# Loads and multiply-adds of the modulation vectors, recorded one step per weight tile of an MLP, with a sixth of the accumulator at a time

## The chip, the cores and the metric

One Trainium2 chip, one of its cores. The time is that of the whole program on the device, in microseconds, the median of several runs.

## The reference

Two blocks of two layers each, in float32, for 512 tokens of width 1024. The first block has an attention with selected keys, a squared-ReLU MLP, an attention with decay, a second MLP. The second block has modulated layers, and its modulation vectors depend on the small input `c` alone, not on the tokens:

```python
cond = jax.nn.silu(c)                                  # [1, 1024]
for i in range(DEPTH):                                 # 2 layers
    mod = cond @ ada_w[i] + ada_b[i]                   # [1024] x [1024, 6144]
    sh1, sc1, g1, sh2, sc2, g2 = jnp.split(mod, N_MOD, axis=-1)
    h = modulate(rmsnorm(x, norm1_g[i]), sh1, sc1)
    ...                                                # attention or gated MLP, added with g1
    h = modulate(rmsnorm(x, norm2_g[i]), sh2, sc2)
    x = x + g2[:, None, :] * sq_relu_mlp_2(h, mlp_w_in[i], mlp_w_out[i])
def sq_relu_mlp(xn, w_up, w_down):
    return jnp.square(jax.nn.relu(xn @ w_up)) @ w_down
```

`ada_w[i]` is 1024 x 6144 float32, 24 MB for each layer: as much as 48 weight tiles of the products.

## The kernel before

**Layout.** The activations lie with the features on the 128 partitions and the 512 tokens along the row: `h` is eight tiles of 128 x 512. A product is computed by weight tiles of 128 output features (`fm`): one load `wr` of 512 KB on SP's queue, a split of it in a high part `wh` (ScalarE) and a low part `wl` (VectorE), then 24 matmuls (8 slices of the inputs, three products each) into one bank of PSUM. There are two buffers `wr` and three each of `wh` and `wl`.

**An MLP** (`mlp`) has 64 such tiles, in four chunks: eight up tiles, then eight down tiles that use them. Behind an up tile VectorE evacuates the bank (`t`: ReLU times 1/rms), ScalarE squares it (`a`) and takes its high part (`ah`), VectorE its low part (`al`). A down tile's 24 matmuls go through the eight `ah`, `al` of the chunk in order, so its last three need those of the chunk's last up tile. Behind a down tile VectorE adds the bank to `h`.

**The modulation vectors.** `ada(0)` is handed to the MLP of the first layer, `ada(1)` to that of the second, as `side`. For each sixth `q` of the 6144 columns and each of eight slices `k` of the 1024 rows, it loads 512 KB (`adaw`, two buffers) on SP's queue; VectorE multiplies its two halves of 512 columns by `silu(c)` (a factor of each partition) and adds them to the accumulator `ada`, 128 x 6144. When all is added up, TensorE transposes the accumulator in 48 pieces of 128 columns, four to a bank `po`, and VectorE sums each bank over the partitions into `mod` (12 sums of 128 x 4). The vectors are used in the second block only.

**What sets the order.** The program is first recorded (`Sched.record`), each instruction with a number, its place in the record plus a bias (`later(n)` adds n). `Sched.order` then plays a list schedule with fixed durations: each engine, whenever it is free in that play, starts the ready instruction of the lowest number; one that needs a tile waits until a buffer of it is free. The instructions are emitted in that order and each engine's queue runs strictly in it; SP's queue holds all loads. On the chip an engine waits at its next instruction until its inputs are there, even where a later one could go. The instructions of `side` are recorded ahead of the MLP's first tile, with a bias of 1600: they give way to some 51 weight tiles.

Of the kernel before, what the change touches and what calls it, by code (L numbers as in the profile page):

```python
# [14 lines left out]
ALU = mybir.AluOpType  # L15
AX = mybir.AxisListType
PSUM = bass.MemoryType.PSUM

P = 128          # partitions, tokens of a block, features of a tile
S = 512          # tokens  # L20
D = 1024
HALVES = slice(0, S // 2), slice(S // 2, S)
KD = D // P      # feature tiles of the model width
NB = S // P      # token blocks
# [7 lines left out]
# columns of the packed per-feature vectors  # L32
# [10 lines left out]
class View:  # L43
    """a part of a tile that is not placed yet; slices and reshapes are replayed on the real one"""
# [33 lines left out]
    def bitcast(self, *a):  # L78
        """to a type of the same size"""
        return View(self.tile, self.steps + (("bitcast", a, {}),), self.box, self.flat)  # L80
# [30 lines left out]
class VPool:  # L111
    def __init__(self, sched, name, bufs, space, before, below):
        self.sched, self.name, self.bufs, self.space = sched, name, bufs, space
        self.before = before      # pools whose room it takes over
        self.below = below
        self.left = 0             # operations not emitted yet
        self.shared = None
        self.open_ = None
        self.slots = {}
# [5 lines left out]
# ns from the end of an instruction to the start of one that needs it  # L125
# [28 lines left out]
class Sched:  # L154
    """Records the program, orders each engine's instructions by a list schedule
    (ready instruction of lowest number first), then emits them in that order."""
# [28 lines left out]
    @contextmanager  # L185
    def later(self, n):
        """instructions that give way to the next n of the program"""
        self.bias += n
        yield
        self.bias -= n  # L190

    @contextmanager
    def after(self):
        """instructions that wait for the one before them"""
        self.gate = len(self.ops) - 1
        yield
        self.gate = None

    def record(self, eng, name, args, kw):
# [17 lines left out]
        if name == "matmul":  # L217
            # the sums of a bank one after the other
            t = outs[0].tile
            if kw["start"]:  # L220
                preds.update(t.sums)
            t.sums = {o.i}
# [19 lines left out]
    def cost(o, outs, ins):  # L242
        """ns that the engine is held, and ns until the result is there"""
# [29 lines left out]
    def order(self):  # L273
# [7 lines left out]
        parked = []               # wait for pools to be shut  # L281
# [23 lines left out]
        def room(p, q):  # L305
            if not q["free"]:
                return False
            # the first slot of a tag is its own, the others are shared by all tags of the pool
            return p.shared is None or not q["used"] or p.shared > sum(max(0, x["used"] - 1) for x in p.slots.values())
# [11 lines left out]
        while ev:  # L321
# [11 lines left out]
            while again:  # L333
                again = False
                for e, heap in ready.items():
                    while heap and busy[e] <= now:
# [15 lines left out]
                        if e == "tensor":  # L352
                            # the array runs at half its clock for a while after a pause
                            if now - busy[e] > 2500:
                                cold = now + 4000
                            if now < cold:
                                dur *= 2
# [62 lines left out]
class Norm:  # L420
    """h / rms(h) * gs + sh in two parts, by halves of the tokens; twice: of h / rms(h) * g_final"""
# [8 lines left out]
    def add(self, k, c=slice(0, S)):  # L430
        """the squares of a tile of h (times the gain) to their sums"""
# [5 lines left out]
        if half and c != self.part:  # L437
            # the squares of a half take turns in the halves of a tile
            self.part, self.n, self.sq = c, 0, net.t(net.np_, "sq", [P, S], bufs=1)
# [13 lines left out]
    def split(self, c):  # L453
# [10 lines left out]
        if self.twice:  # L464
            # 1/rms(h) / rms(h / rms(h) * g) = (mean((h g)^2) + eps (mean(h^2) + eps))^-1/2
            m2 = net.t(net.np_, "m2", [P, 2])
            nc.vector.tensor_scalar(m2, ms, EPS, 1.0, ALU.mult, ALU.mult)
            nc.vector.scalar_tensor_tensor(m2, ps[:, n + 4 : n + 8 : 2], 1.0 / D, m2, ALU.mult, ALU.add)
            nc.gpsimd.tensor_tensor(r, m2, net.mhalf[:, :2], ALU.pow)
            with net.sched.later(1000):  # L470
                nc.gpsimd.tensor_tensor(self.r[:, b0 : b0 + 2], ms, net.mhalf[:, :2], ALU.pow)
        else:
            nc.gpsimd.tensor_tensor(r, ms, net.mhalf[:, :2], ALU.pow)
# [16 lines left out]
class Net:  # L490
    def __init__(self, ctx, tc, I, out, stop=None):
# [6 lines left out]
        self.pp.shared = 4        # and a bank for each of 4 tags  # L498
# [34 lines left out]
    def weight(self, src, n):  # L533
        """src: [128, n] in DRAM; returns its high and low part"""
# [18 lines left out]
    def fm(self, src, xh, xl, w=None):  # L553
        """one tile of 128 output features, all tokens"""
# [8 lines left out]
    def tm(self, src, xh, xl, evac, banks=("mm", "mm", "lg", "tp")):  # L563
        """a strip of output features with the tokens on partitions; src: [u, 128, kk, n]"""
# [17 lines left out]
    def squares(self, col=None):  # L582
        """sums of the squares of h (times a gain) over the features: [token, 2 * block]"""
# [16 lines left out]
    def rms(self):  # L600
        """1/rms of the columns of h: [token, block], and spread over all partitions"""
# [35 lines left out]
    def last(self, src, xh, xl, gate, norm):  # L637
        """the product that completes h, and the norm of h; the end of both goes by halves of the tokens"""
# [20 lines left out]
    def first(self, src, xh, xl):  # L659
        """the first three tiles of a product, by halves of the tokens"""  # L660
# [13 lines left out]
    def mlp(self, xh, xl, w_up, w_down, rb=None, gate=None, side=None, norm=None):  # L674
        nc = self.nc
        with self.tc.tile_pool(name=self.name("mlp"), bufs=2) as mp:
            if side is not None:
                with self.sched.later(1600):
                    side(mp)
            head = [] if rb is not None else self.first([w_up[j] for j in range(3)], xh, xl)  # L680
            for c in range(DFF // D):
                ah, al = [], []
                for j in range(KD):
# [12 lines left out]
                    al.append(l_)  # L696
                if c < DFF // D - 1:
                    for k in range(KD):
                        self.residual(k, self.fm(w_down[c, k], ah, al), gate)
                else:  # L700
                    self.last([w_down[c, k] for k in range(KD)], ah, al, gate, norm)

# [1 line left out]
    def rope(self, pool, ps, cos, sin, eng, n=P, q=None, ceng=None):  # L704
        """ps * cos + (its halves of each head exchanged) * sin, in SBUF; the first n rows, repeated"""
# [14 lines left out]
    def stacks(self, pool, tag, s, bufs=None):  # L720
        """for the two heads of s: [high; low] and [low; high] along the partitions"""
# [9 lines left out]
    def doubles(self, pool, tag, s, scale):  # L731
        """for the two heads of s, scaled: [high; high] and [low; low]"""
# [13 lines left out]
    def softmax(self, pool, npr, lhs, rhs, W, masks, extra, rows, on_act=False):  # L746
        """rows of probabilities of one head, block after block; W: block of queries to its number of keys;
        lhs, rhs: pairs of operands whose products add up to the logits; rows: a factor of each row of them;
        on_act: which engine divides by the sums"""
# [32 lines left out]
    def turned(self, pool, nth, pr, W, b):  # L782
        """the probabilities of the keys of block b with the keys on partitions, in two parts, and their columns"""
# [16 lines left out]
    def heads(self, pool, npr, nth, lhs, rhs, v, o, masks=None, extra=(None, None), causal=True, rows=(None, None), blocks=range(NB), narrow=False, on_act=False):  # L800
        """two heads: their softmax times v, one above the other, in two parts to o.
        narrow: the products of the parts of v one after the other, not in the two halves of the array's columns"""
# [32 lines left out]
    def half_out(self, w, o, c):  # L835
        """adds the product of o for half of the tokens to h"""
# [11 lines left out]
    def layer_a(self, first):  # L848
# [6 lines left out]
        with ExitStack() as c1:  # L855
# [7 lines left out]
            # scores of the keys, then what is added to the logits  # L863
# [7 lines left out]
            with tc.tile_pool(name="ai", bufs=2) as ip:  # L871
# [37 lines left out]
                def top(i):  # L909
                    """keeps the 128 largest scores of each row: the others get NEG"""  # L910
# [38 lines left out]
    def layer_b(self):  # L949
# [4 lines left out]
        with ExitStack() as c1:  # L954
# [30 lines left out]
            with tc.tile_pool(name="bc", bufs=1) as bp:  # L985
                # log(sigmoid(z)) = min(z, 0) - log(1 + exp(-|z|)), and its sums over the tokens so far
# [60 lines left out]
    def layer_c(self, x, gate, norm):  # L1047
# [8 lines left out]
        with ExitStack() as c1:  # L1056
# [14 lines left out]
            def inverse(ps, st):  # L1071
                """1/rms of each of the two heads of a tile: [token, 2 * block + head]; by way of the bank st"""
# [140 lines left out]
    def ada(self, i):  # L1213
        nc, I = self.nc, self.I

        def side(pool):
            acc = self.t(pool, "ada", [P, 6 * D], bufs=1)
            for q in range(6):
                for k in range(KD):
# [3 lines left out]
                    for s in (0, 512):  # L1223
                        a = acc[:, q * D + s : q * D + s + 512]
# [4 lines left out]
            m = self.mod[i]  # L1229
            for j in range(0, 48, NB):  # L1230
                ps = self.po()
                for b in range(NB):
                    nc.tensor.transpose(ps[:, b * P : (b + 1) * P], acc[:, (j + b) * P : (j + b + 1) * P], self.ident)
                nc.vector.tensor_reduce(m[:, j : j + NB], ps.rearrange("p (b k) -> p b k", b=NB), AX.X, ALU.add)
# [105 lines left out]
def _layout(a):  # L1340
    """the inputs as the program reads them: tiled, permuted, packed"""

    def fm(w, kk=8):
        """[K, N] to [K/(128 kk), N/128, 128, kk, 128]"""
        k, n = w.shape
        return w.reshape(k // (P * kk), kk, P, n // P, P).transpose(0, 3, 2, 1, 4)

    def tm(w, kk, n):
        """[1024, N] to [N/n, 8/kk, 128, kk, n]"""
# [69 lines left out]
```

## Time and profile before

| | |
|---|---|
| median of 3 runs | 2642.7 us (2639.9 to 2642.72) |
| profiled execution | its span is 2640.9 us, first to last instruction; no other time of it is given |
| busy, share of the span | VectorE 1577.0 us (60%), ScalarE 1159.9 us (44%), GpSimd 467.8 us (18%) |
| mean granted TensorE clock | 0.990 |
| hardware DMA queue | 290.18 MB |

The profile is of one execution; its start times are microseconds from the first instruction. A group of a view names output and inputs as `out<-in`; all instructions have line 413, that of the emitting loop, so they are told apart by their tiles. `PE` is TensorE's matmul, `DVE` VectorE, `ACT` ScalarE, `SPq` the queue of the loads. The MLP with `ada(0)` begins near 265 us, that with `ada(1)` near 890 us.

### The profile page before, as it was taken

To read this page: it belongs to the slowest core of one execution; us is meant where nothing else is said; L and a number is where in the kernel's file an instruction comes from. 1 tells how busy PE (TensorE), PEld (TensorE's weight loads), DVE (VectorE), ACT (ScalarE), POOL (GpSimd) and SP (SyncE) were. 2 spreads that over 40 slices of the span, in tenths; PEclk is the share of its full clock that TensorE was granted. 3 is DMA by queue.
4 is the path that set the end of the run, shared out by engine and by line. 5 is a ranking of instruction groups with operands and counts; after the bars stand their busy time and mean duration, and the time that the engine had idled before them with its cause. 6 is when DMAs were issued, how large, how long until landed. Compare 5 with 4: busy or idle time off the path is not lost.

```text
span 2640.9 us, 34588 instructions
## 1 busy us (share of the span) xinstructions
PE 2570.4 (97%) x12998; PEld 2173.2 (82%) x12998; DVE 1577.0 (60%) x2667; ACT 1159.9 (44%) x2096; POOL 467.8 (18%) x628
## 2 busy tenths in 40 slices
PE   8989998999999998999999999999999999999999
PEld 6769787888888886888876888888998888888887
DVE  7998875455468777435698544434546654644433
ACT  5678322334477423323687433323435443523322
POOL 3773000000075000000686200000202210200000
PEclk9999999999999999999999999999999999999999
DMA  4222784223231576222211132222333332222222
GB/s 148 87 69 84 253 263 142 96 88 108 88 89 57 190 253 210 98 99 84 96 47 35 65 110 98 96 96 88 99 108 120 103 100 90 87 103 96 96 97 95
DMA packets 92056, 292.39 MB, mean 111 GB/s; under 512 B 11760, under 2 KB 16112, under 8 KB 91888
## 3 DMA queue, kind: packets, MB, share of 16 engines
q1 hardware_dynamic: 91888, 290.18, 32.8%
q8 instruction: 102, 1.67, 0.2%
q14 instruction: 66, 0.54, 0.1%
HBM read 277.28 MB, written 2.10 MB: 106 GB/s over the span
## 4 chain that ended last, share of the span: by engine, by line
PE 75%; DVE 10%; DMA 8%; ACT 3%; issue 2%; POOL 2%; SPq 0%; DVEq 0%; ACTq 0%; POOLq 0%
PE mm L413 64%; DMA adaw<-in_ada_w 7%; PE lg L413 4%; PE tp L413 4%; PE po L413 3%; DVE ada L413 2%; DVE mask L413 1%; DVE st L413 1%; ACT pr L413 1%; DVE tl L413 1%; POOL pr L413 1%; DVE m L413 1%; DVE acc L413 1%; ACT st L413 1%; ACT th L413 1%
## 5 line engine op out<-in xcount | busy, mean ns | idle before, releaser
L413 ACT ACTIVATE wh<-wr 128x1024 fp32r<-128x1024 f32 (+2 forms) x480 | 449.0, 940 | 1047.1 <-PE mm L413 865.3
L413 PE MATMUL mm<-xh,wh 128*128 128x512 f32 (+1 forms) x1640 | 627.8, 384 | 7.4 <-ACT wh L413 7.2
L413 DVE TENSOR_TENSOR wl<-wr,wh 128x1024 fp32r<-128x1024 f32 (+1 forms) x382 | 452.4, 1185 | 303.2 <-ACT wh L413 297.1
L413 PE MATMUL mm<-xh,wl 128*128 128x512 f32 (+1 forms) x1640 | 627.2, 383 | 1.3 <-DVE wl L413 0.9
L413 PE MATMUL mm<-xl,wh 128*128 128x512 f32 (+1 forms) x1640 | 627.0, 383 | 0.6 <-POOL xl L413 0.4
L413 PE MATMUL mm<-ah,wh 128*128 128x512 f32 (+1 forms) x1072 | 409.4, 382 | 16.9 <-ACT ah L413 16.9
L413 PE MATMUL mm<-al,wh 128*128 128x512 f32 (+1 forms) x1072 | 409.9, 382 | 0.7 <-DVE al L413 0.7
L413 PE MATMUL mm<-ah,wl 128*128 128x512 f32 (+1 forms) x1072 | 408.8, 381 | 1.1 <-DVE wl L413 1.1
L413 PEld LDWEIGHTS mm<-xh,wh 128*128 128x128 f32 x1640 | 311.6, 190 | 61.5 <-ACT wh L413 7.2
L413 PEld LDWEIGHTS mm<-xh,wl 128*128 128x128 f32 x1640 | 312.0, 190 | 59.7 <-DVE wl L413 3.5
L413 PEld LDWEIGHTS mm<-xl,wh 128*128 128x128 f32 x1640 | 312.5, 191 | 55.7 <-POOL xl L413 1.2
L413 PEld LDWEIGHTS mm<-ah,wh 128*128 128x128 f32 x1072 | 202.6, 189 | 58.3 <-ACT ah L413 20.0
L413 PEld LDWEIGHTS mm<-al,wh 128*128 128x128 f32 x1072 | 202.6, 189 | 41.2 <-DVE al L413 3.0
L413 PEld LDWEIGHTS mm<-ah,wl 128*128 128x128 f32 x1072 | 202.8, 189 | 39.9 <-DVE wl L413 2.0
L413 DVE SCALAR_TENSOR_TENSOR h<-mm,mod,h 128x512 f32<-128x512 f32 (+1 forms) x113 | 79.7, 707 | 260.3 <-PE mm L413 260.2
L413 POOL TENSOR_TENSOR wl<-wr,wh 128x512 fp32r<-128x512 f32 x98 | 133.1, 1368 | 144.9 <-ACT wh L413 138.4
L413 DVE SCALAR_TENSOR_TENSOR ada<-adaw,cs,ada 128x512 f32<-128x512 f32 x168 | 119.0, 748 | 43.2 <-DMA adaw<-in_ada_w 42.4
L413 DVE TENSOR_TENSOR h<-mm,h 128x512 f32<-128x512 f32 (+1 forms) x91 | 56.5, 624 | 147.0 <-PE mm L413 147.0
L413 PE MATMUL tp<-ident,pr 128*128 128x128 f32 x576 | 115.0, 278 | 7.3 <-POOL pr L413 3.4
L413 POOL TENSOR_SCALAR pr<-pr,rs 128x512 f32<-128x512 f32 (+3 forms) x168 | 110.3, 667 | 48.4 <-DVE rs L413 34.5
L413 ACT ACTIVATE ah<-a 128x512 fp32r<-128x512 f32 x128 | 80.9, 632 | 83.7 <-DVE a L413 81.6
L413 POOL TENSOR_TENSOR r<-ms,mhalf 128x2 f32<-128x2 f32 (+1 forms) x10 | 9.3, 934 | 606.9 <-DVE ms L413 545.7
(259 smaller groups left out, 4087.6 us busy)
## 6 DMA issues: line engine op xcount, KB each, us to landing
adaw<-in_ada_w SPq DMA_DIRECT2D x96, 512.0 KB, 4.5
wr<-in_w_up SPq DMA_DIRECT2D x64, 512.0 KB, 3.5
wr<-in_w_down SPq DMA_DIRECT2D x64, 512.0 KB, 3.5
wr<-in_w_in SPq DMA_DIRECT2D x64, 512.0 KB, 3.4
wr<-in_w_out SPq DMA_DIRECT2D x64, 512.0 KB, 3.5
wr<-in_w_gu SPq DMA_DIRECT2D x24, 512.0 KB, 3.5
wr<-in_w_gv SPq DMA_DIRECT2D x32, 384.0 KB, 3.0
wr<-in_w_go SPq DMA_DIRECT2D x32, 384.0 KB, 2.9
```

Of the source, the lines that this page charges most:

```text
L413: getattr(getattr(self.nc, o.eng), o.name)(*args, **kw)
```

## The change

`side` becomes a generator. Each step of it is one load `adaw` with its two multiply-adds; the last step of a sixth also has the transposes and sums of that sixth. `mlp` runs one step behind each of its tiles 1 to 55 (counted from 1), but not behind each eighth, so the steps are recorded between the tiles and get their numbers, with no bias. That makes 49 calls, for 48 steps and the short end (bias and gains). The accumulator `ada` is 128 x 1024, for one sixth, and there are two of them (the pool's `bufs=2`), where there was one of 128 x 6144. Comments are removed elsewhere.

```diff
     def mlp(self, xh, xl, w_up, w_down, rb=None, gate=None, side=None, norm=None):
         nc = self.nc
         with self.tc.tile_pool(name=self.name("mlp"), bufs=2) as mp:
-            if side is not None:
-                with self.sched.later(1600):
-                    side(mp)
+            side = None if side is None else side(mp)
+            tiles = 0
+
+            def step():
+
+                nonlocal tiles
+                tiles += 1
+                if side is not None and tiles % 8:
+                    next(side, None)
+
             head = [] if rb is not None else self.first([w_up[j] for j in range(3)], xh, xl)
...
                     ah.append(h_)
                     al.append(l_)
+                    step()
                 if c < DFF // D - 1:
                     for k in range(KD):
                         self.residual(k, self.fm(w_down[c, k], ah, al), gate)
+                        step()
                 else:
+                    for _ in side or ():
+                        pass
                     self.last([w_down[c, k] for k in range(KD)], ah, al, gate, norm)
...
         def side(pool):
-            acc = self.t(pool, "ada", [P, 6 * D], bufs=1)
+            m = self.mod[i]
             for q in range(6):
+                acc = self.t(pool, "ada", [P, D])
                 for k in range(KD):
...
-                        a = acc[:, q * D + s : q * D + s + 512]
+                        a = acc[:, s : s + 512]
...
-            m = self.mod[i]
-            for j in range(0, 48, NB):
-                ps = self.po()
-                for b in range(NB):
-                    nc.tensor.transpose(ps[:, b * P : (b + 1) * P], acc[:, (j + b) * P : (j + b + 1) * P], self.ident)
-                nc.vector.tensor_reduce(m[:, j : j + NB], ps.rearrange("p (b k) -> p b k", b=NB), AX.X, ALU.add)
+                    if k < KD - 1:
+                        yield
+                for j in range(0, KD, NB):
+                    ps = self.po()
+                    for b in range(NB):
+                        nc.tensor.transpose(ps[:, b * P : (b + 1) * P], acc[:, (j + b) * P : (j + b + 1) * P], self.ident)
+                    o = q * KD + j
+                    nc.vector.tensor_reduce(m[:, o : o + NB], ps.rearrange("p (b k) -> p b k", b=NB), AX.X, ALU.add)
+                yield
```

## Rows read from the trace of the kernel before

**Rows 1.** The page: TensorE's busy time; the chain of waits by line; the loads.
```profile
PE 2570.4 (97%) x12998; PEld 2173.2 (82%) x12998; DVE 1577.0 (60%) x2667; ACT 1159.9 (44%) x2096; POOL 467.8 (18%) x628
...
PE mm L413 64%; DMA adaw<-in_ada_w 7%; PE lg L413 4%; PE tp L413 4%; PE po L413 3%; DVE ada L413 2%; DVE mask L413 1%; DVE st L413 1%; ACT pr L413 1%; DVE tl L413 1%; POOL pr L413 1%; DVE m L413 1%; DVE acc L413 1%; ACT st L413 1%; ACT th L413 1%
...
adaw<-in_ada_w SPq DMA_DIRECT2D x96, 512.0 KB, 4.5
```

**Rows 2.** Windows of 20 us: length, busy us (instructions) by engine, clock, DMA.
```profile
300.00:320.00 20.00, 17.46 (x76) 13.92 (x75) 15.86 (x22) 7.26 (x10) 0.00 (x0) 1.00 0.78 248
400.00:420.00 20.00, 12.74 (x41) 8.56 (x40) 16.89 (x23) 6.74 (x9) 0.00 (x0) 0.74 0.66 210
420.00:440.00 20.00, 20.00 (x90) 16.56 (x89) 5.85 (x7) 3.52 (x4) 0.00 (x0) 1.00 0.28 104
...
1020.00:1040.00 20.00, 12.41 (x47) 8.47 (x45) 16.85 (x23) 7.51 (x11) 0.00 (x0) 0.84 0.66 214
```

**Rows 3.** VectorE's timeline, quiet part: start us, length us, instruction [idle before].
```profile
461.66 0.69 DVE L413 SCALAR_TENSOR_TENSOR t<-mm,y 128x512 f32<-128x512 f32 x1 [3.34 <-PE mm L413]
...
548.70 0.69 DVE L413 SCALAR_TENSOR_TENSOR t<-mm,y 128x512 f32<-128x512 f32 x1 [3.34 <-PE mm L413]
```

**Rows 4.** VectorE's timeline: `t` of tiles 1, 7, 23; then 1, 7, 32.
```profile
277.90 0.69 DVE L413 SCALAR_TENSOR_TENSOR t<-mm,y 128x512 f32<-128x512 f32 x1 [0.36 <-PE mm L413]
...
315.52 0.68 DVE L413 SCALAR_TENSOR_TENSOR t<-mm,y 128x512 f32<-128x512 f32 x1
...
412.98 0.68 DVE L413 SCALAR_TENSOR_TENSOR t<-mm,y 128x512 f32<-128x512 f32 x1
...
903.05 0.68 DVE L413 SCALAR_TENSOR_TENSOR t<-mm,y 128x512 f32<-128x512 f32 x1
...
939.50 0.68 DVE L413 SCALAR_TENSOR_TENSOR t<-mm,y 128x512 f32<-128x512 f32 x1
...
1086.25 0.69 DVE L413 SCALAR_TENSOR_TENSOR t<-mm,y 128x512 f32<-128x512 f32 x1 [3.35 <-PE mm L413]
```

**Rows 5.** TensorE's timeline at the end of tile 8, in both MLPs.
```profile
314.87 0.39 PE L413 MATMUL mm<-ah,wl 128*128 128x512 f32 x1
...
318.64 0.39 PE L413 MATMUL mm<-ah,wl 128*128 128x512 f32 x1
...
939.87 0.39 PE L413 MATMUL mm<-ah,wl 128*128 128x512 f32 x1
...
942.62 0.39 PE L413 MATMUL mm<-ah,wl 128*128 128x512 f32 x1
```

**Rows 6.** Instructions on the tile `ada`: one group; windows (PE, PEld, DVE).
```profile
L413 DVE SCALAR_TENSOR_TENSOR ada<-adaw,cs,ada x168: 736/747/754, 271.2 to 1036.8; 128x512 f32<-128x512 f32 x168
...
260.00:315.50 55.50, 0.00 (x0) 0.00 (x0) 20.07 (x30) 1.00 0.76 254
315.50:363.50 48.00, 0.00 (x0) 0.00 (x0) 21.50 (x33) 1.00 0.81 263
```

**Rows 7.** Longer windows of the first MLP; last columns clock, DMA share, GB/s.
```profile
265.00:317.00 52.00, 50.26 (x230) 41.36 (x228) 43.38 (x62) 21.52 (x29) 1.48 (x1) 1.00 0.77 253
317.00:396.00 79.00, 77.84 (x341) 63.92 (x341) 60.48 (x84) 19.89 (x24) 0.00 (x0) 1.00 0.80 260
...
417.00:563.00 146.00, 146.00 (x640) 120.79 (x640) 58.98 (x66) 41.04 (x49) 0.53 (x1) 0.99 0.27 96
```

**Rows 8.** Waits, 255 to 430 us: us in total, times, longest; then SP's queue.
```profile
DVE ada L413 <- DMA adaw<-in_ada_w: 25.7, 29, 1.8
...
SPq L413 <- DVE ada L413: 64.0, 46, 2.1
```

**Rows 9.** TensorE's transposes of `ada`: the group; two of its timeline.
```profile
L413 PE MATMUL po<-ident,ada x96: 270/272/275, 564.8 to 1205.1; 128*128 128x128 f32 x96
...
573.07 0.60 PE L413 MATMUL po<-ident,ada 128*128 128x128 f32 x4
...
573.74 0.60 PE L413 MATMUL po<-ident,ada 128*128 128x128 f32 x4
```

## The prediction

> **What bounds the kernel now.** I began with the page: TensorE is busy for 97% of the span, and the chain of waits is 64% product matmuls, but 7% of it is the loads `adaw` of the modulation weights [rows 1]. So the windows came next, to see where TensorE is not full. In a quiet 20 us it starts 90 matmuls with no idle time; the only windows inside the two first MLPs that fall well short are at 300, 400, 940 and 1020 us, the second and the last with a granted clock under 1 (940 is as 300 and not shown) [rows 2]. Those are the stretches where `adaw` arrives.
>
> VectorE's timeline says how much they cost. In quiet parts one weight tile follows the other at a fixed pace: from the evacuation `t` of tile 32 (461.66) to that of tile 48 (548.70) it is 87.04 us, 5.44 a tile [rows 3]. Counting tiles of an MLP from 0 (0-7 up, 8-15 down, and so on), tile 1 of the first MLP is evacuated at 277.90 with no lag. At 5.44 a tile, tile 32 would be due at 277.90 + 31 x 5.44 = 446.54; it comes at 461.66. So the first MLP loses 15.1 us before tile 32. In the second, 903.05 + 168.64 = 1071.69 against 1086.25: 14.6 us [rows 4]. Both together, 29.7 us, are all that the stage can give back; after it TensorE is full.
>
> Where is it lost? At two tiles, not evenly: where an up part ends and the down part needs its last activations. The first is tile 8. `t` of tile 7 comes at 315.52, due at 277.90 + 6 x 5.44 = 310.54, so VectorE lags by 4.98 us; in the second MLP 939.50 against 935.69, 3.81 us [rows 4]. TensorE, at 0.227 us a matmul, would have started the third matmul after 314.87 at 315.55 and does so at 318.64: 3.09 us lost; in the second MLP 942.62 against 940.55, 2.07 us [rows 5]. So about 1.8 us of lag is absorbed and the rest is lost one for one. What is left, 15.1 - 3.1 = 12.0 and 14.6 - 2.1 = 12.5 us, is lost around tile 24: `t` of tile 23 comes at 412.98 [rows 4], 12 us behind its pace, and the clock falls after the wait.
>
> Why the lag? In this stage VectorE's order holds two loads (four multiply-adds of 0.75 us) per tile: 30 of these operations start before `t` of tile 7, 33 more in the next eight tiles [rows 6]. Two `adaw` and one weight, 512 KB each [rows 1], are 1.57 MB, which at the 253 to 260 GB/s of these stretches [rows 7] take 6.1 us, more than 5.44. VectorE stands at a multiply-add whose load has not landed (25.7 us in the first MLP) with `t` and `wl` behind it, and SP's queue in turn waits 64.0 us for those multiply-adds to free a buffer [rows 8]. From 417 us on DMA is at 27% and VectorE busy for 59 us in 146 [rows 7]: room that nothing uses.
>
> **The change, part by part.**
>
> *Order of recording.* The steps get the numbers of tiles 1 to 55 instead of a number 1600 later. But the scheduler starts whatever is ready, and a load needs only a buffer; numbers decide only between ready instructions. So nothing holds a step to its tile. What does hold it is the accumulator: before, one tile for all six sixths was free from the start; now there are two tiles of a sixth each. The first two sixths (16 loads) can run as soon as the pool opens, at the same two per tile: tiles 0 to 7 stay as they are. I cost this part at nothing, and expect the 3.1 and 2.1 us at tile 8 to stay. For the first three tiles the steps outrank a later `wl`; one load is 1.5 us of VectorE, so this may add 0 to 1.5 us of lag at tile 8.
>
> *Two accumulators.* The third sixth needs the first one's transposes. They have the number of the ninth tile (tile 8), and TensorE, always full, runs them behind its matmuls. So sixths 3 to 6 are freed after tiles 8, 17, 26 and 35 (steps 8, 16, 24 and 32, with every eighth tile skipped), and each then runs as a burst of eight loads over four tiles: 9-12, 18-21, 27-30, 36-39. In a burst VectorE falls behind as before: 4.98 us in six tiles or 3.81 in six, 0.64 to 0.83 a tile, so 2.5 to 3.3 us in four. The first and third burst are in down tiles (9-12, 27-30), where nothing urgent waits for the evacuation. The second ends two tiles before tile 24; in tiles without loads VectorE is busy for 40% of the time (59 of 146 us [rows 7]), so it makes up some 3 us a tile and its lag is gone by then: the 12.0 and 12.5 us go. The fourth ends right at tile 40, where another up part ends: 2.5 to 3.3 less the 1.8 absorbed is 0.7 to 1.5 us lost. But two loads are there already when the burst starts, which takes off up to one tile's lag: 0 to 0.9. I take 0.6 for each MLP.
>
> *Transposes and sums.* As many as before (96 transposes [rows 9] and 24 sums, in both MLPs); they move from tiles 53-56 to the ends of six tiles. Four and one matmul take 0.67 us from 573.07 to 573.74 [rows 9], so (0.67 - 0.23)/4 = 0.11 us each, 5.3 us an MLP, before as after. Eight in a row instead of singles between matmuls: by the same rows no dearer; up to 0.03 more each would be 1.4 us an MLP, and no less than 0. I take 0. The sums of VectorE before a burst's first multiply-add wait for TensorE behind `t` of the same tile, in time that VectorE has to spare.
>
> *Loads and multiply-adds.* 48 loads and 96 operations an MLP, same sizes; none added. What is late next is the product itself, 5.44 us a tile.
>
> **The sum.** Saved: 12.0 + 12.5. Given back: 2 x 0.6. Net 23.3 us. The profiled span of 2640.9 becomes 2617.6. The median of the runs is 2642.7, 1.8 above that span, so I forecast 2642.7 - 23.3 = 2619.4 us.
>
> **Rivals.**
>
> *Evenly spread, no loss left.* If the loads really come one per tile, the tile's two transfers (0.524 MB at 256 GB/s, 2.05 us each) fit in 5.44 us and no lag builds up, tile 8 has no wait either, and the whole 29.7 us comes back: 2613.0. For: the recording puts one step per tile. Against: a load that is ready is not held back.
>
> *Half of it returns.* If the third sixth follows the first 16 loads with hardly a pause (tile 8 ends just where the sixteenth load is used up), or a burst packs three loads in a tile, VectorE enters the next boundary late. Half of the 24.5 us would be lost again: 2642.7 - 12.3 = 2630.4. For: the lag at tile 8 is largest just there. Against: six tiles without loads between bursts.
>
> *Slower: VectorE held at the accumulator.* The first multiply-add of sixths 3 to 6 waits for TensorE's transposes, and what stands behind it in VectorE's queue (`t`, `wl`, then ScalarE's `ah` and TensorE itself) waits too. If it stands one tile too early, each of the eight waits costs 5.44 - 1.8 = 3.6 us, 29 in all, more than the 24.5 saved: 2647.4. It decides from about 3.1 us lost at each (24.5 / 8). For: VectorE already stands in front of late loads that way [rows 8]. Against: the transposes stand right behind the tile that is being computed, their inputs ready for tiles, and VectorE has work of that same tile ahead of them. The skill ("TensorE: Matmul & The Clock Gate", "Architectural detail") calls VectorE's queue strictly first in, first out, on which this rival rests; the waits in the trace agree.
>
> *The change does nothing.* If the lag came from VectorE's own work and not from the transfers, or the order stayed at two loads a tile to the end, the waits would return at tiles 24 or 40: 2642.7. For: VectorE is busy for 43 of 52 us there. Against: that leaves 9 us, and the transfers alone need 6.1 us a tile [rows 7]. The Trainium skill ("DMA: Bandwidth & Descriptors", section "Specifications") puts a core's limit on HBM at about 358 GB/s; by an estimate from that the three loads take 4.4 us and fit in a tile, the transfers would not be the cause, and this rival would hold. The stretches with `adaw` stay at 260 and below, so the trace speaks against it.
>
> **How the numbers follow.** Forecast 0.58, evenly spread 0.14, half returned 0.13, slower 0.07, nothing 0.08. A run tells a change from none at about 0.2%, 5.3 us. Faster: 0.58 + 0.14 + 0.13 = 0.85; same 0.08; slower 0.07. The range: the best case 2613.0, with a microsecond for the spread of the runs, to the half-returned case 2630.4 with the extra lag at tile 8 (1.5 in each MLP): 2612 to 2633. Outside are the last two cases and a little at the bottom, under 2 in 10. The forecast's own range, with 0 to 1.5 us at tile 40, 0 to 1.5 at tile 8 and 0 to 1.4 for the transposes in each MLP, is 2618 to 2627.
>
> **What would show it.** In the profile after: `adaw` in a first run of 16 loads, then groups of eight with pauses, over some 215 us an MLP instead of 155; the window at 300 still short by about 3 us, those around tile 24 (400 and 1020 us) full and at clock 1.00; transposes in eights after tiles 8, 17, 26, 35, 44 and 53; the pace of 5.44 unchanged. Wrong would be: a TensorE wait at tile 24 of over 2 us, VectorE waiting at `ada` for TensorE rather than for a load, or no wait at tile 8.

## The result and the profile after

The changed kernel takes 2618.25 us (median of 4 runs, 2612.38 to 2622.34), the kernel before beside it 2641.3 us (4 runs, 2636.75 to 2642.72). The ratio is 0.9913, with an interval of 0.9894 to 0.9932: 23.05 us less, where 23.3 were forecast (2619.4 us). The profiled execution of after took 2612.38 us with a span of 2610.6, so it is the fastest of its four.

The page of after: engines; the chain of waits by line; the loads' time to landing.

```profile
PE 2556.0 (98%) x12998; PEld 2167.4 (83%) x12998; DVE 1576.0 (60%) x2667; ACT 1160.0 (44%) x2096; POOL 468.9 (18%) x628
...
PE mm L413 72%; PE lg L413 4%; PE tp L413 4%; PE po L413 3%; DMA adaw<-in_ada_w 2%; DVE mask L413 1%; DVE st L413 1%; DVE tl L413 1%; ACT pr L413 1%; POOL pr L413 1%; DVE m L413 1%; DVE acc L413 1%; ACT st L413 1%; DVE ada L413 0%; DVE y L413 0%
...
adaw<-in_ada_w SPq DMA_DIRECT2D x96, 512.0 KB, 4.5
```

Against [rows 1], the same instructions and the same landing time of a load; but the loads hold 2% of the chain instead of 7%, and the products 72% instead of 64%.

Windows of 20 us of after, columns as in [rows 2]:

```profile
300.00:320.00 20.00, 20.00 (x94) 16.63 (x93) 16.88 (x25) 7.93 (x10) 0.00 (x0) 1.00 0.79 260
400.00:420.00 20.00, 20.00 (x94) 16.64 (x93) 10.08 (x14) 5.00 (x6) 0.00 (x0) 1.00 0.24 79
1020.00:1040.00 20.00, 20.00 (x94) 16.67 (x93) 10.43 (x15) 3.18 (x3) 0.00 (x0) 1.00 0.47 154
```

The windows at 400 and 1020 us are full and at a clock of 1.00, as forecast. The one at 300 is full too, which was not.

VectorE's timeline of after, `t` of tiles 2, 7 and 23 of the first MLP, then of tiles 1, 7 and 23 of the second:

```profile
284.24 0.68 DVE L413 SCALAR_TENSOR_TENSOR t<-mm,y 128x512 f32<-128x512 f32 x1
...
311.46 0.68 DVE L413 SCALAR_TENSOR_TENSOR t<-mm,y 128x512 f32<-128x512 f32 x1
...
399.82 0.69 DVE L413 SCALAR_TENSOR_TENSOR t<-mm,y 128x512 f32<-128x512 f32 x1 [2.69 <-PE mm L413]
...
888.54 0.69 DVE L413 SCALAR_TENSOR_TENSOR t<-mm,y 128x512 f32<-128x512 f32 x1
...
925.45 0.68 DVE L413 SCALAR_TENSOR_TENSOR t<-mm,y 128x512 f32<-128x512 f32 x1
...
1012.44 0.69 DVE L413 SCALAR_TENSOR_TENSOR t<-mm,y 128x512 f32<-128x512 f32 x1 [2.69 <-PE mm L413]
```

The brackets are what to read: in [rows 4] tile 23 had none, VectorE came to it late. Now VectorE has been idle for 2.69 us before it and waits for TensorE: no lag is left there. At tile 7 the MLPs differ. In the first, 311.46 - 284.24 = 27.22 us are five tiles of 5.44 us, so no lag builds up. In the second, 925.45 - 888.54 = 36.91 against 6 x 5.44 = 32.64: 4.3 us late, much as before the change (3.81).

TensorE's waits for the weights and activations of the MLPs between 255 and 1220 us, in total, times and longest; first before, then after:

```profile
PE mm L413 <- ACT ah L413: 16.9, 6, 4.4
PE mm L413 <- DVE wl L413: 2.1, 5, 0.7
```

```profile
PE mm L413 <- ACT ah L413: 1.8, 1, 1.8
...
PE mm L413 <- ACT wh L413: 1.1, 1, 1.1
PE mm L413 <- DVE al L413: 0.5, 2, 0.2
```

One wait for `ah` is left. It is that at tile 8 of the second MLP, here in TensorE's timeline of after, with the first sixth's transposes right behind it:

```profile
927.52 0.49 PE L413 MATMUL mm<-ah,wh 128*128 128x512 f32 x1 [1.76 <-ACT ah L413]
928.24 0.50 PE L413 MATMUL mm<-al,wh 128*128 128x512 f32 x1 [0.23 <-DVE al L413]
...
928.82 1.04 PE L413 MATMUL po<-ident,ada 128*128 128x128 f32 x8
929.61 0.47 PE L413 MATMUL mm<-ah,wh 128*128 128x512 f32 x1
```

1.76 + 0.23 = 1.99 us lost, 2.07 in [rows 5]. The eight transposes hold TensorE from 928.82 to 929.61, 0.10 us each.

The waits alone are not the whole loss at tile 24. Before, those of TensorE from 390 to 430 us are 6.5 us for `ah` and 1.2 for `wl`, 7.7 of the 12.0 us. Behind them the granted clock was at the lower of its two levels, 1.2 GHz:

```profile
410.00:415.00 5.00, 0.72 (x2) 0.00 (x1) 3.99 (x6) 1.26 (x2) 0.00 (x0) 0.50 0.71 233
```

From 415 to 420 us it was still 0.58, and matmuls came 0.43 us apart instead of 0.227. Much of the rest of the 12.0 us goes with this clock, so taking the wait away also gives back what stands behind it.

What the loads do now is in the windows of the tile `ada` alone (PE, PEld, DVE, then clock, DMA share, GB/s), first MLP:

```profile
380.00:400.00 20.00, 0.00 (x0) 0.00 (x0) 5.65 (x8) 1.00 0.78 255
400.00:420.00 20.00, 1.03 (x8) 0.94 (x8) 0.92 (x3) 1.00 0.24 79
420.00:440.00 20.00, 0.00 (x0) 0.00 (x0) 9.60 (x14) 1.00 0.82 273
440.00:460.00 20.00, 0.00 (x0) 0.00 (x0) 0.00 (x0) 1.00 0.43 146
```

Bursts with pauses: 14 operations in one window, none in the next, and the eight transposes of a sixth where a burst becomes free. The last multiply-add of `ada(0)` is past 480 us, before it was near 415.

Last, where the time came from. The sums of squares `ms` of the next norm stand at the end of each MLP and can be compared; before, then after:

```profile
L413 DVE TENSOR_SCALAR ms<-po x1: 163/163/163, 640.3 to 640.3; 128x4 f32<-128x4 f32 x1
...
L413 DVE TENSOR_SCALAR ms<-po x1: 161/161/161, 895.5 to 895.5; 128x4 f32<-128x4 f32 x1
...
L413 DVE TENSOR_SCALAR ms<-po x2: 159/159/159, 1255.1 to 1270.4; 128x2 f32<-128x2 f32 x2
```

```profile
L413 DVE TENSOR_SCALAR ms<-po x1: 163/163/163, 625.4 to 625.4; 128x4 f32<-128x4 f32 x1
...
L413 DVE TENSOR_SCALAR ms<-po x1: 161/161/161, 881.0 to 881.0; 128x4 f32<-128x4 f32 x1
...
L413 DVE TENSOR_SCALAR ms<-po x2: 159/160/160, 1228.8 to 1243.8; 128x2 f32<-128x2 f32 x2
```

At 640.3 the changed kernel is 14.9 us ahead, 1.6 of which it already had at 230 us, before any of the change: 13.3 us are the first MLP's (forecast 12.0 - 0.6 = 11.4). From 895.5 to 1255.1 it is 359.6 against 347.8: 11.8 us are the second's (forecast 12.5 - 0.6 = 11.9). Together 25.1. The rest of the 30.3 us between the two spans lies in stages whose instructions are the same, ahead of the first MLP and behind the second, and no row here explains it; the four runs of the changed kernel alone spread over 10 us.

### The profile page after: what moved, and what is told of

It is laid out like the page before. It is cut to its first block, busy times and chain, and to the rows that moved or that the text cites. A ratio compares the mean times of both kernels' runs of the same rounds, so it can differ in the third digit from the quotient of the medians.

```text
span 2610.6 us, 34572 instructions
## 1 busy us (share of the span) xinstructions
PE 2556.0 (98%) x12998; PEld 2167.4 (83%) x12998; DVE 1576.0 (60%) x2667; ACT 1160.0 (44%) x2096; POOL 468.9 (18%) x628
## 4 chain that ended last, share of the span: by engine, by line
PE 82%; DVE 9%; ACT 3%; DMA 2%; POOL 2%; issue 2%; SPq 0%; DVEq 0%; ACTq 0%; POOLq 0%
PE mm L413 72%; PE lg L413 4%; PE tp L413 4%; PE po L413 3%; DMA adaw<-in_ada_w 2%; DVE mask L413 1%; DVE st L413 1%; DVE tl L413 1%; ACT pr L413 1%; POOL pr L413 1%; DVE m L413 1%; DVE acc L413 1%; ACT st L413 1%; DVE ada L413 0%; DVE y L413 0%
## 5 line engine op out<-in xcount | busy, mean ns | idle before, releaser
L413 DVE TENSOR_TENSOR al<-a,ah 128x512 fp32r<-128x512 f32 x128 | 88.2, 691 | 45.3 <-ACT ah L413 45.3
```

The source lines that it names most:

```text
L413: getattr(getattr(self.nc, o.eng), o.name)(*args, **kw)
```

## Experiments

Medians against the kernel before, which ran beside each group on the same chip (2639.42 us beside e1 to e4, 2639.35 beside e5 to e8, 2640.59 beside e9 to e12):

| run | what differs | us | ratio, interval |
|---|---|---|---|
| e1_acc6 | changed kernel, six accumulators | 2634.28 | 0.998, 0.9971 to 0.9989 |
| e2_acc3 | three | 2618.14 | 0.9916, 0.9902 to 0.9929 |
| e3_acc1 | one | 2614.34 | 0.9903, 0.9889 to 0.9916 |
| e4_gated | two, each step held to its tile | 2611.57 | 0.9894, 0.988 to 0.9907 |
| e11_gated_again | the same | 2612.65 | 0.99, 0.9884 to 0.9917 |
| e5_numbers | two, the old numbers of the MLP | 2617.14 | 0.9913, 0.9899 to 0.9926 |
| e10_gated_numbers | e4 and e5 together | 2611.12 | 0.9888, 0.9873 to 0.9903 |
| e8_after_again | changed kernel | 2615.27 | 0.9906, 0.9891 to 0.9922 |
| e12_after_third | changed kernel | 2616.51 | 0.9914, 0.9899 to 0.9929 |
| e6_halfload | kernel before, loads of half the size (half of the weights is left out) | 2611.25 | 0.9892, 0.9878 to 0.9905 |
| e7_halfwork | kernel before, multiply-adds of half the width (half of the sums is left out) | 2620.66 | 0.9929, 0.9916 to 0.9941 |
| e9_buf4 | kernel before, four buffers for the loads | 2611.81 | 0.9894, 0.9879 to 0.9909 |

### Do the accumulators pace the loads, or the recording? (e1_acc6)

```diff
-                acc = self.t(pool, "ada", [P, D])
+                acc = self.t(pool, "ada", [P, D], bufs=6)
```

> The changed kernel with six accumulators of a sixth instead of two; recording, numbers and instructions are the same. Theory A (the two accumulators hold the loads back, the recording order does not): VectorE's order goes back to four multiply-adds a tile up to tile 23, so the wait of TensorE at tile 24 returns in both MLPs, some 12 us in the second and 10 in the first (where the first eight tiles now hold 13 loads and not 15); granted clock under 1 there; about 2640 us, between 2636 and 2644. Rival B (recording a step with each tile spreads the loads): as the changed kernel, about 2618 us, and no wait at tile 24.

Windows of 20 us at tile 24 of both MLPs, and TensorE's timeline there:

```profile
400.00:420.00 20.00, 14.56 (x51) 10.69 (x50) 16.56 (x23) 6.61 (x9) 0.00 (x0) 0.83 0.79 262
1020.00:1040.00 20.00, 15.55 (x59) 12.09 (x58) 15.65 (x21) 6.75 (x9) 0.00 (x0) 0.83 0.54 188
```

```profile
412.98 0.79 PE L413 MATMUL mm<-ah,wh 128*128 128x512 f32 x1 [4.76 <-ACT ah L413]
...
1034.76 0.80 PE L413 MATMUL mm<-ah,wh 128*128 128x512 f32 x1 [4.45 <-ACT ah L413]
```

Recorded one step per tile, but with an accumulator for each sixth, the loads run at two a tile up to tile 23 again, and the wait at tile 24 is back with the clock's fall behind it. So the recording does not spread the loads; the two accumulators do. The kernel is 5.1 us faster than before, though, where it was expected level, and lies below the range given. Two things may be part of it: two sixths are transposed by tile 24, inside the lag (16 x 0.11 = 1.8 us an MLP), and the first MLP has fewer loads in its up part (see e5). Neither was tested, so the cause of these 5 us is open. Of the 24.1 us of e8 and e12, then, about 19 hang on there being only two accumulators.

### Three accumulators and one (e2_acc3, e3_acc1)

```diff
-                acc = self.t(pool, "ada", [P, D])
+                acc = self.t(pool, "ada", [P, D], bufs=3)
```

> Three accumulators. Theory A: loads run on through tile 15, pause, and then come in fours a tile for tiles 18 to 21 only; VectorE's lag from the first run lies in down tiles (8 to 15) and two tiles without loads follow, so no wait over 0.5 us at tile 24 and 2618 us, between 2615 and 2622, as with two. Rival C (the loss grows with how far the loads may run ahead): a quarter of the way to six accumulators, about 2624 us. Rival B: 2618 us as well.

The time is that of two. TensorE's timeline at tile 24 of the first MLP:

```profile
407.39 0.50 PE L413 MATMUL mm<-ah,wh 128*128 128x512 f32 x1 [1.25 <-ACT ah L413]
```

That wait was to be under 0.5 us. The pause expected at tiles 16 and 17 does not come either: VectorE's timeline has four or five multiply-adds in every tile from 8 to 21, so the first run goes over into the next. It ends some two tiles ahead of tile 24, and its lag is not quite gone there. Loads at two a tile up to tile 21 thus leave TensorE a wait of 1.25 us, up to tile 23 those of 7.7 us of before: what counts is how far ahead of a boundary they end.

```diff
-                acc = self.t(pool, "ada", [P, D])
+                acc = self.t(pool, "ada", [P, D], bufs=1)
```

> One accumulator of a sixth. Theory A: only eight loads before tile 8, over tiles 0 to 3 or 4, so the wait at tile 8 in the second MLP (about 2 us in the changed kernel) goes; none is left elsewhere: 2616 us, between 2612 and 2619. Rival D (VectorE held at the accumulator until TensorE's transposes, with the evacuations behind it): five waits an MLP instead of four, and the lag of a burst that ends at tile 40 or 48 comes out: 2620 us or more, with VectorE idle in front of a first product until TensorE.

TensorE's waits for the weights and activations of the MLPs, 255 to 1220 us, of the kernel with one accumulator, and what ended VectorE's idle time before the instructions on `ada`:

```profile
PE mm L413 <- ACT wh L413: 1.1, 1, 1.1
```

```profile
DVE ada L413 <- DMA adaw<-in_ada_w: 22.2, 35, 2.1
```

With one, each sixth waits for the transposes of the sixth before it, the tightest form of the rival in which VectorE is held at the accumulator. It does not happen: VectorE is idle at `ada` for loads only, TensorE has no wait for `ah` or `al` in either MLP, and the time is no longer than with two. That rival falls.

### A step truly held to its tile (e4_gated, e11_gated_again, e8_after_again, e12_after_third)

`after()` makes the instructions in it wait, in the planned order, for the last one recorded ahead of them.

```diff
-                    next(side, None)
+                    with self.sched.after():
+                        next(side, None)
```

> The changed kernel, but in the planned order each step waits for its own tile (a dependency of the plan alone), so that VectorE's order holds one load, two multiply-adds, per tile. Theory A with the transfers as the cause of the lag: two transfers of 512 KB a tile, 4.1 us at 256 GB/s, fit in 5.44; no wait of TensorE at tiles 8, 24, 40 or 56 over 0.5 us, VectorE waits for a load less than 10 us in all; 2616 us, between 2612 and 2619. Rival E (the steps cost something wherever they stand, so an even spread loses a little at each tile): above 2622 us.

The window of tiles 8 to 23 of the first MLP, against [rows 7]:

```profile
317.00:396.00 79.00, 79.00 (x358) 65.55 (x357) 48.97 (x64) 22.82 (x28) 0.00 (x0) 1.00 0.50 176
```

DMA at 176 GB/s, VectorE busy for 49 of 79 us, TensorE full: this is the rival "evenly spread", and 2611.57 us is near the 2613.0 priced for it (just under the range expected). The changed kernel isn't this. Repeated side by side, without another edit:

> The changed kernel once more, beside the others of this call: 2618 us, between 2612 and 2624. In the first MLP no wait of TensorE at tile 8 or 24, in the second about 2 us at tile 8.

> One load per tile in the plan, once more, beside the changed kernel of this call: 2611 us, between 2608 and 2615, 3 to 8 us below the changed kernel (its 2 us wait at tile 8 of the second MLP, and what the clock loses behind it).

> The changed kernel beside the others of this call: 2616 us, between 2612 and 2622.

Changed 2615.27 and 2616.51, gated 2612.65 us; both repeats of the changed kernel have the wait at tile 8 of the second MLP (2.14 + 0.23 and 2.07 + 0.22 us). Side by side (e11, e12) the gated one is 3.9 us below, with no run of the one within the other's range. The wait is 2.3 us of that. The clock behind it is a part too, as the windows at 930 us show, e12 and then after:

```profile
930.00:935.00 5.00, 4.90 (x19) 4.22 (x19) 3.80 (x7) 1.06 (x1) 0.00 (x0) 0.66 0.45 173
```

```profile
930.00:935.00 5.00, 5.00 (x24) 4.10 (x23) 4.16 (x7) 0.00 (x0) 0.00 (x0) 1.00 0.52 179
```

Five matmuls fewer in 5 us are some 1.1 us. In e8 the clock is 0.66 there as well; in the profiled execution of after, where the wait was 1.76 us, it stayed at 1.00.

### Why tile 8 of the first MLP lost its wait (e5_numbers, e10_gated_numbers)

In after, the half product of the attention ahead of the first MLP (`half_out`, recorded with a bias of 1000) ends later: its last `h` at 273.79 us instead of 266.45, behind the MLP's tile 0, and the first product of `ada` comes at 277.2 instead of 269.2. The theory: the 207 instructions of `side` no longer stand ahead of the MLP's first tile, so this tile has a lower number and outranks the end of the half product. The edit gives the MLP its old numbers back:

```diff
+            if side is not None:
+                self.sched.bias += 207
             side = None if side is None else side(mp)
```

> The changed kernel with 207 added to all numbers from the first MLP on, as many as the instructions that stood ahead of the MLP's first tile before; so against the last tiles of the attention's first half product, which carry a bias of 1000, the MLP's first tiles rank as before. Theory F (in the first MLP the wait at tile 8 went only since these numbers put the attention's last tile behind the MLP's first, which starts the loads some 8 us later): the first load's product is back near 269 us, the 3 us wait at tile 8 of the first MLP returns in part, 1 to 3 us, the 1.1 us wait of TensorE near 274 us goes; time 2618 to 2621 us, a difference that the times alone can't tell. Rival G (two accumulators made it go): no wait at tile 8 of the first MLP here either.

TensorE's timeline at tile 8 of the first MLP:

```profile
313.85 0.51 PE L413 MATMUL mm<-ah,wh 128*128 128x512 f32 x1 [1.42 <-ACT ah L413]
314.58 0.50 PE L413 MATMUL mm<-al,wh 128*128 128x512 f32 x1 [0.22 <-DVE al L413]
```

The first product of `ada` is back at 266.3 us, the wait at tile 8 is back with 1.42 + 0.22 us, and the wait of 1.1 us for `wh` that after had at the MLP's start is gone. The theory holds, for about half of the 3.1 us that were lost there before; why the wait does not come back whole was not traced. Gain and loss nearly cancel, and 2617.14 us, just under the range expected, is not to be told from the changed kernel's time.

With steps held to their tiles and the old numbers:

> One load per tile in the plan, and 207 added to the numbers from the first MLP on. Neither edit leaves a wait that the trace names in the MLPs: TensorE's 1.1 us wait near 274 us goes too. 2610 us, between 2607 and 2614; against one load per tile alone (2611.6 us) a gain of 0 to 2 us, which the times can hardly tell.

2611.12 us, with no wait of TensorE for a weight or an activation of either MLP: the lowest median of the study, though not to be told from e4, e6 or e9.

### What makes the loads slow: transfers, VectorE, or the two buffers? (e6_halfload, e7_halfwork, e9_buf4)

All three are the kernel before, with the order of every engine unchanged. First half the bytes, with VectorE's work as it was:

```diff
-                    nc.sync.dma_start(w, I["ada_w"][i, k, :, q * D : (q + 1) * D])
+                    nc.sync.dma_start(w[:, :512], I["ada_w"][i, k, :, q * D : q * D + 512])
...
-                            nc.vector.scalar_tensor_tensor(a, w[:, s : s + 512], c, a, ALU.mult, ALU.add)
+                            nc.vector.scalar_tensor_tensor(a, w[:, :512], c, a, ALU.mult, ALU.add)
```

> The kernel before, the same order of instructions on every engine, but each load of the modulation weights brings 512 columns of 1024 and both multiply-adds use them (half of the weights is left out). Theory H (the transfers make the lag): 2 x 0.26 + 0.52 MB a tile are 4.1 us at 256 GB/s, VectorE's wait for loads falls from 25.7 us to under 8 in the first MLP, the waits at tiles 8 and 24 go, all 29.7 us come back: 2612 us, between 2609 and 2618. Rival I (VectorE's own work makes the lag): waits at tile 24 stay over 5 us an MLP, 2630 us or more.

The window of tiles 8 to 23, what VectorE waits for (255 to 430 us), and the loads' times to landing:

```profile
317.00:396.00 79.00, 79.00 (x350) 65.43 (x349) 68.99 (x94) 23.49 (x29) 0.00 (x0) 1.00 0.60 192
```

```profile
DVE ada L413 <- DMA adaw<-in_ada_w: 0.8, 2, 0.4
...
DMA to landing us min/median/max: 2.7/3.0/5.1
```

VectorE does all its work at two loads a tile, is busy for 69 of 79 us and keeps up. So VectorE's own work was not the bound. Then half the work, with the bytes as they were:

```diff
-                            nc.vector.scalar_tensor_tensor(a, w[:, s : s + 512], c, a, ALU.mult, ALU.add)
+                            nc.vector.scalar_tensor_tensor(a[:, :256], w[:, s : s + 256], c, a[:, :256], ALU.mult, ALU.add)
```

> The kernel before, the same order, full loads, but each multiply-add after a sixth's first works on 256 of its 512 columns (the rest of the sums is left out), so VectorE has some 1.2 us less of work a tile. Theory H (the transfers make the lag): VectorE only waits longer for its loads, some 45 us instead of 25.7 in the first MLP, and the lag stays: 2636 us or more. Rival I (VectorE's own work): the lag goes and with it 20 us or more: under 2622 us.

The same window, TensorE's timeline at tile 24 of both MLPs, and the times to landing:

```profile
317.00:396.00 79.00, 79.00 (x351) 65.40 (x350) 50.98 (x87) 21.81 (x26) 0.00 (x0) 1.00 0.83 270
```

```profile
406.02 0.80 PE L413 MATMUL mm<-ah,wh 128*128 128x512 f32 x1 [4.39 <-ACT ah L413]
...
1019.23 0.50 PE L413 MATMUL mm<-ah,wh 128*128 128x512 f32 x1 [1.19 <-ACT ah L413]
```

```profile
DMA to landing us min/median/max: 3.7/4.7/6.6
```

I expected at least 2636 us if the transfers alone set the pace, and that was missed by 15: with every byte still moved, 18.7 us of the loss are gone and the rate rises from 260 to 270 GB/s. Neither transfers alone nor VectorE alone explain both runs; a loop in which the two add up does. A buffer is refilled only when VectorE has read it, so with two buffers and two loads a tile, a tile can't be shorter than one load's landing plus its two multiply-adds. Before: 4.5 [rows 1] + 2 x 0.747 [rows 6] = 6.0 us, measured 6.16 (21 tiles, 283.68 to 412.98). With half the work (0.480 us a multiply-add): 4.7 + 2 x 0.480 = 5.7, measured 5.82 (the same 21 tiles). With half the load: 3.0 + 1.5 = 4.5, under 5.44, so no lag. The test is to leave work and bytes alone and give the loop more buffers:

```diff
-            tag, bufs = (self.tag, self.bufs) if p.shared is None else ("all", p.shared + len(p.slots))
+            tag, bufs = (self.tag, 4 if self.tag == "adaw" else self.bufs) if p.shared is None else ("all", p.shared + len(p.slots))
```

> The kernel before, the same order of instructions on every engine, but four buffers behind the loads `adaw` instead of two (the plan still counts two). Theory J (the lag is that of the loop of two buffers: a load can only start when VectorE has used an earlier one, so VectorE's time adds to the transfer's; the bare transfers need less): SP waits far less for the multiply-adds (64.0 us before in the first MLP, under 25 now), the rate of the stage rises from 253-260 GB/s to 270 or more, the pace from 6.1 us a tile to 5.6-5.8, the waits at tile 8 go below 1 us and those at tile 24 below 5: 2620 us, between 2614 and 2626. Rival H (the transfers alone, at 260 GB/s, set the pace): rate and pace stay, 2636 us or more.

100 us of the first MLP, before and then with four buffers:

```profile
290.00:390.00 100.00, 97.46 (x429) 80.20 (x428) 77.60 (x108) 27.89 (x35) 0.00 (x0) 1.00 0.80 257
```

```profile
290.00:390.00 100.00, 100.00 (x443) 82.80 (x442) 87.80 (x121) 32.28 (x40) 0.00 (x0) 1.00 0.81 292
```

With four buffers, the longest of the waits of SP's queue (255 to 430 us), the loads' times to landing, and VectorE's `t` of tiles 2 and 23:

```profile
SPq L413 <- DVE wl L413: 127.9, 33, 5.0
```

```profile
DMA to landing us min/median/max: 3.8/5.6/7.9
```

```profile
283.86 0.68 DVE L413 SCALAR_TENSOR_TENSOR t<-mm,y 128x512 f32<-128x512 f32 x1
...
397.96 0.68 DVE L413 SCALAR_TENSOR_TENSOR t<-mm,y 128x512 f32<-128x512 f32 x1
```

The same order, bytes and work go at 292 GB/s instead of 257. SP's queue no longer waits for the multiply-adds at all (what is left is the wait for `wl`, the last reader of a weight's buffer), each load lands later (5.6 us against 4.5), and the pace is 5.43 us a tile (283.86 to 397.96, 21 tiles). That is TensorE's own pace, so 292 GB/s is no limit of the transfers either: 1.57 MB in 5.44 us are 289 GB/s. The wait at tile 24 is gone and not only shorter, and the time is below the range expected. The loop was the cause, and this one edit of the kernel before gives 28.8 us, more than the change (e12, in the same group, 24.1).

## Why the prediction was right, step by step

**Where the time was lost** held: two waits, at tiles 8 and 24; the most that any run won, 29.5 us (e10), is about the 29.7 that the rows allowed. **That recording per tile does not spread the loads, and that the accumulators do,** held, down to the bursts (e1, and the windows of `ada`). **The 12.0 and 12.5 us at tile 24** came back: no wait is left there in either MLP, and the `ms` rows show the gain to within 0.7 us in each. **Transposes at no extra cost** held: 0.10 us each in a row of eight, 0.11 with the slower matmul behind them, 0.11 costed.

**Tile 8** held in the second MLP (1.99 us, 2.1 forecast) and failed in the first, where 3.1 us were to stay and none did, which the prediction had named as a sign of being wrong. I had followed the numbers of the steps, but not those of the tiles behind the place that the steps left: 207 lower, they changed ranks with the attention's half product; e5 shows it for 1.64 of the 3.1 us, the rest is open. VectorE now runs the multiply-adds of eight and a half loads between `t` of tile 2 and of tile 7, where it ran ten, at an unchanged 3.2 us a load (27.22 / 8.5; before 31.84 / 10), and that just fits. The new wait of 1.1 us at the MLP's start takes part of it back.

**Tile 40**, 0.6 us in each MLP, cost nothing; no wait of TensorE is there. The rows allowed 0 as the lower end.

**The cause of the lag** was wrong, though the forecast did not hang on it. I read 253 to 260 GB/s as what the DMA can give ([rows 6] even has 263), and so "the transfers alone need 6.1 us a tile". They don't: e9 moves the same at 289 to 296 GB/s. The rate was a result of the loop, not its limit. The Trainium skill ("DMA: Bandwidth & Descriptors", section "Specifications") gives a higher limit for a core, and I weighed it as a reason for the rival in which the change does nothing. My estimate from that limit said that the transfers were not the cause, and e9 bears that out, though its 296 GB/s stay below the limit. The conclusion that the change would then do nothing did not follow: fewer loads per tile shorten the lag whatever makes a load slow. The row that could have told me was in front of me: SP's 64.0 us of waits for `ada` [rows 8] is the loop's return path, and landing plus multiply-adds, 4.5 + 1.5 us, is the tile that was measured. That wait alone proves nothing, since e6 has 49.1 us of it and loses nothing; the sum is what decides.

The misses do not cancel: + 3.1 - 1.1 at the first tile 8 and + 1.2 at tile 40 are gains of 3.2 us over the forecast, of which the `ms` rows show 25.1 - 23.3 = 1.8. That the medians differ by 23.05 us, so close to 23.3, is in part luck: the runs of the changed kernel spread over 10 us, and e8 and e12 gave 24.1.

## What to carry to other kernels

Ask which resource holds a step back in the planned order (a buffer, an accumulator, a gate); the place in the record moves only ties, and moving a block of records also moves the rank of whatever stood behind it. Before reading a stretch's GB/s as a limit, add landing time and consumer time and divide by the number of buffers: if that is the pace, more buffers are the cheaper edit than a new order. Work beside a saturated engine is placed well when each burst ends some tiles ahead of the next point where that engine needs the helper without delay.

## What the runs showed of the hardware

The DMA engines' busy share was 0.80 at 257 GB/s and 0.81 at 292 (the two windows of 100 us above): that share told nothing of the room left. With four buffers instead of two, a load of 512 KB landed later, 5.6 us against 4.5, while the rate rose by 14%. Where the clock fell in the stretches looked at, TensorE had just waited, but the length of one wait did not settle it. It was 0.83 in the windows of e1 with waits of 4.8 and 4.5 us, and 0.66 from 930 to 935 us behind the waits of 2.1 us of e8 and e12. It was 1.00 from 320 to 325 us behind the wait of 2.3 us at tile 8 in the first MLP of the kernel before, and in all windows of after shown here, whose longest wait was 1.8 us.
